# SSM quarters reordered, u and y stored in the chain's layout, gate weights on GpSimd's queue: a hybrid encoder block on Trainium2

## The chip, the cores and the metric

The kernel runs on one core of one Trainium2 chip. A core has five engines, each with an instruction stream of its own that it works through in order: TensorE (PE: matmuls and transposes, with its weight loads listed as PEld), VectorE (DVE), ScalarE (ACT), GpSimd (POOL) and SyncE (SP, which here only issues DMAs). ACT and POOL can issue DMAs too. The metric is the device time of one execution in microseconds; lower is better.

## What is computed

One encoder layer over 16 meta tokens and 1024 inputs of width 1024 (L = 1040 rows), in float32. The part that the change touches is the state-space branch ("SSM") and the sigmoid gates beside it:

```python
xn = _rmsnorm(h, norm_mix_g)
q, k, v, f_logit, u, gates = jnp.split(xn @ w_in, SPLITS, axis=-1)
y_a = _forgetting_attention(q, k, v, f_logit, b_forget) @ w_attn_out
z = jax.nn.gelu(_s5(u, ...))              # 32 groups of 16 channels, 64 complex states each
zg = z @ w_glu
y_s = zg[..., :D_MODEL] * sigmoid(zg[..., D_MODEL:])
g = sigmoid(gates)
h = h + (g[..., :D_MODEL] * y_a + g[..., D_MODEL:] * y_s) @ w_o
h = h + _conv_ffn(_rmsnorm(h, norm_ffn_g), ...)
out = _rmsnorm(h, norm_final_g)[:, N_META:]

def _s5(u):                               # x_t = lam_bar * x_(t-1) + b_bar u_t,  y = Re(C x_t) + D u_t
    _, states = lax.associative_scan(combine, (a, bu), axis=0)
    return einsum('gcp,lbgp->blgc', cmat, states).real + d_skip * u
```

## The kernel before

Every float32 matrix product is made of float32r pieces: an operand is split into a rounded part (`hi`) and the rest (`lo`), and three products are summed (`dense_steps`, L139 to L143). A weight block of 1024 x 128 passes `wchunk` (L127): one load into `raw` by SP, a rounding copy to `whi`, and a subtraction to `wlo` on GpSimd (`split_lo`, L124). With `act=True` the rounding copy is ACT's (L133).

The program is written in a tile framework. The code's order is a priority; a planner with its own estimates of durations makes each engine's final order before the run, and adds the semaphores. A tile with a tag has a fixed number of buffers (`bufs`), and a new tile of that tag waits until an older one is done with. A pool that is closed gives its SBUF to later pools, whose tiles wait for those that they lie on. `after(inst, first)` orders two instructions on one engine.

In order of time, the part of the kernel up to the attention does this:

1. Rows are normalised (`norm_rows`, L152), transposed on PE and split into `xhi` and `xlo` (`to_feature`, L162). The square of each row tile is ACT's (L155), as is the copy into `xhi` (L169).
2. `u_proj` (L300) projects u, 128 channels at a time, from weights split in `u_weights` (L263), and stores it to DRAM as `u_d`, [512 channels, 8, 130]: a sequence of 1040 rows is 130 chunks of CH = 8 rows.
3. `ssm` (L1176) first works out powers and rotations in small DVE steps, then does four quarters of 8 groups each. For quarter q, `tables(q)` (L1426) makes Gm (DVE), Kt (PE, then ACT copies it, L1448), Tm (Kt sent eight times by SP into a Toeplitz form, L1456, after GpSimd cleared it, L1454) and Wi (DVE, PE, ACT). `chain(q)` (L1474) loads U from `u_d` in eight pieces (SP, L1482), multiplies by Wi (L1489), ACT copies the result to wr and wi (L1492, L1493), DVE rotates, scans (L1504, L1505) and rotates back into St, PE makes Y from Tm and U (L1522) and from Gm and St (L1523), ACT copies Y out, applies GELU (L1526) and issues eight stores to `y_d` (L1528).
4. `gate_chunk` (L344) makes the sigmoid gates of the SSM branch, eight chunks of 72 matmuls, each result of 128 x 1026 stored to `g_d` by ACT (L361). These matmuls are what PE can do while the quarters go round.
5. `load_z` (L434) reads `y_d` back, one load of 128 channels each (SP, L439), splits z and makes the sums and differences that the GLU's products use (L444 to L462; GpSimd makes one of them, L455).
6. `project_qk(0)` (L375) and `forget` (L409, with weights loaded in `forget_w`, L324) run on PE, then the GLU (`glu`, L465, whose products are in `seven`, L175, at L194 to L196).

After that come values, attention, the output projection and the feed-forward part, which the change does not touch.

The order of step 3 in the code is `tables(0)`, `chain(0)`, `tables(1)`, `chain(1)`, then `u_proj(2)`, and the same for quarters 2 and 3 (L314 to L336). In a chain the wr and wi copies come first and the output last, so in the code the copies of quarter q+1 come behind the output of quarter q.

Of the kernel before, what the change touches and what calls it, by code (L numbers as in the profile page):

```python
# [47 lines left out]
def block_kernel(ctx, tc, x, meta, g1, w_in, b_f, w_ao, l_re, l_im, b_re, b_im, c_re, c_im,  # L48
# [78 lines left out]
    def wchunk(src, k, eng=None, act=False):  # L127
        raw = wp.tile([P, k, P], F, tag="raw", name="raw", padded_shape=[P, KD, P])
        SY.dma_start(raw, src.rearrange("(k p) m -> p k m", p=P))
        hi = wp.tile([P, k, P], R, tag="whi", name="whi", padded_shape=[P, KD, P])  # L130
        lo = wp.tile([P, k, P], R, tag="wlo", name="wlo", padded_shape=[P, KD, P])
        if act:
            S.copy(hi, raw)  # L133
# [18 lines left out]
    def norm_rows(pl, src, n, gB, xs):  # L152
        sq = pl.tile([P, D], BF, tag="sq", name="sq")
        ss = pl.tile([P, 1], F, tag="ss", name="ss", bufs=3)
        S.activation(sq[:n], src, AF.Square, accum_out=ss[:n])  # L155
        va = pl.tile([P, 1], F, tag="vr", name="vr", bufs=3)
        v_ = V.tensor_scalar(va[:n], ss[:n], 1.0 / D, EPS, ALU.mult, ALU.add)
        rs = pl.tile([P, 1], F, tag="rs", name="rs", bufs=3)
        GP.tensor_tensor(rs[:n], va[:n], nhalf[:n], ALU.pow)
        return v_, V.scalar_tensor_tensor(out=xs[:n], in0=src, scalar=rs[:n], in1=gB[:n], op0=ALU.mult, op1=ALU.mult)  # L160

    def to_feature(xs, n, dhi, dlo, col, bank=st_ps):  # L162
        for hf in range(2):
# [5 lines left out]
            S.copy(ho, t3[:, :, :n])  # L169
            split_lo(V, dlo[:, 4 * hf:4 * hf + 4, col:col + n], t3[:, :, :n], ho)  # L170

    def m_ps():
# [101 lines left out]
    S.dma_start(g1B, g1.partition_broadcast(P))  # L274
    ssm_log, ssm_loads, ssm_steps = ssm(tc, sp, st_ps, ident, u_d, y_d, l_re, l_im, b_re, b_im, c_re, c_im, d_sk, l_dt)
    xts = [sp.tile([P, D], F, tag=tag, name="xt", bufs=n) for tag, n in (("sy", 3), ("Gm", 2), ("Wi", 2), ("U", 2))
# [23 lines left out]
    def u_proj(m0):  # L300
# [29 lines left out]

    u_proj(2)
    forget_w()
    st_u.close()
    for q in range(2, 4):
        ssm_tables(q)
        ssm_chain(q)  # L336


    st_g = ExitStack()
    gp_ = pool(st_g, "gates", side="right")  # L340

    okeep = {}

    def gate_chunk(i, pl, tanh):  # L344
        c0 = 3 * AW + H + SW + P * i
        whi, wlo = wchunk(w_in[:, c0:c0 + P], KD, GP, act=not tanh)
        gs = pl.tile([P, LQ], F, tag="gs", name="gs", bufs=1 if tanh else 2)
        for t, n in QBLK:
            ps = mm_ps()
            yield from dense_steps(ps[:, :n], whi, wlo, xhi[:, :, T0 + t:T0 + t + n],  # L350
                                   xlo[:, :, T0 + t:T0 + t + n], KD)
            if tanh:
                S.activation(gs[:, t:t + n], ps[:, :n], AF.Tanh, scale=0.5)
            else:
                S.activation(gs[:, t:t + n], ps[:, :n], AF.Sigmoid)
        if tanh:
            GP.tensor_scalar(gs, gs, 0.5, 0.5, ALU.mult, ALU.add)
        if pl is not gp_ and i == KD - 1:
            okeep["g"] = gs
        else:  # L360
            (SY if tanh else S).dma_start(g_d[P * i:P * i + P], gs)  # L361

    for i in range(KD, 2 * KD):
        run(gate_chunk(i, gp_, False))
    st_g.close()
    st_s.close()

# [66 lines left out]
    def load_z():  # L434
        zts = []
        for m in range(4):
            tag = "gl" if m % 2 else "ms"
            zt = gz.tile([P, CH, NCH], F, tag=tag, name="zt", bufs=2)
            SY.dma_start(zt, y_d[P * m:P * m + P])  # L439
            zts.append(zt)  # L440
# [59 lines left out]

    n_used = [0]
    T4 = load_z()
    qk = qk_tiles(0)
    run(project_qk(0, qk))
# [670 lines left out]

def ssm(tc, sp, s_ps, ident, u_d, y_d, l_re, l_im, b_re, b_im, c_re, c_im, d_sk, l_dt):  # L1176
    nc = tc.nc
# [21 lines left out]

    lraw = sm([G, 2, 2, NS])  # L1200
    for i, src in enumerate((l_re, l_im)):
# [24 lines left out]
    def rest():  # L1226
# [21 lines left out]
        def expf(o, a):  # L1248
            n, r, t, e = sm(W), sm(W), sm(W), sm(W, dt=I32)
            TS(n, a, 1.4426950408889634, None, ALU.mult)  # L1250
# [15 lines left out]
        def cmul(or_, oi, ar, ai, br, bi, t, u):  # L1266
# [6 lines left out]
            V.tensor_copy(or_, t)  # L1273

        dt_ = sm(W)
        expf(dt_, ldt)
# [40 lines left out]
        TT(pi[:, 1], rad, ei, ALU.mult)  # L1317
        w1, w2 = sm([P, 4, G]), sm([P, 4, G])
# [107 lines left out]
        def tables(qt):  # L1426
# [47 lines left out]
        def chain(qt):  # L1474
            g0 = qt * GQ
            Gm, Tm, Wi, dt8 = state.pop(qt)
            if qt == 1:
                rot.append(rotation(1))
            rc, rs = (t_[:, qt % 2 * HQ:qt % 2 * HQ + HQ] for t_ in rot[qt // 2])
            U = big("U", [P, GQ, NCH])  # L1480
            for j in range(CH):
                SY.dma_start(U[16 * (7 - j):16 * (8 - j)],  # L1482
                             u_d[g0 * GC:(g0 + GQ) * GC, j, :].rearrange("(g c) n -> c g n", c=GC))
            wr, wi, ta, tb = (big(n, [P, HQ, NCH]) for n in ("wr", "wi", "ta", "tb"))
            for e in range(2):
                for q in range(0, HQ, 2):
# [5 lines left out]
                    S.copy(wr[64 * e:64 * e + 64, q:q + 2], w3[:64])  # L1492
                    S.copy(wi[64 * e:64 * e + 64, q:q + 2], w3[64:])  # L1493
            TT(ta, wr, rc, ALU.mult)
            TT(tb, wi, rs, ALU.mult)
# [13 lines left out]
            for part, (op, fa, fb) in enumerate(((ALU.subtract, wr, ta), (ALU.add, ta, wr))):  # L1509
# [3 lines left out]
                for e in range(2):  # L1513
                    r_ = slice(64 * e, 64 * e + 64)
                    TT(S4[64 * part:64 * part + 64, :, e, 1:], x_[r_, :, :NCH - 1], y_[r_, :, :NCH - 1], op)
            Y = big("sy", [P, GQ, NCH], "Y")
            for q in range(0, GQ, 3):
                nq = min(3, GQ - q)
                yps = s_ps()
                for i in range(nq):  # L1520
                    yo = yps[:, NCH * i:NCH * i + NCH]
                    PE.matmul(yo, Tm[:, q + i, :], U[:, q + i, :], start=True, stop=False)  # L1522
                    PE.matmul(yo, Gm[:, q + i, 1:, :].rearrange("p t c -> p (t c)"), St[:, q + i, :],  # L1523
                              start=False, stop=True)
                S.copy(Y[:, q:q + nq].rearrange("p a n -> p (a n)"), yps[:, :NCH * nq])
            S.activation(Y, Y, AF.Gelu_apprx_tanh)  # L1526
            for j in range(CH):
                S.dma_start(y_d[g0 * GC:(g0 + GQ) * GC, j, :].rearrange("(g c) n -> c g n", c=GC),  # L1528
                            Y[16 * j:16 * j + 16])

# [31 lines left out]
```

## Time and profile before

| | us |
|---|---|
| median of 3 runs | 1583.6 |
| lowest and highest | 1581.55, 1585.9 |
| the profiled execution's own time | 1581.32 |
| its span in the profile | 1579.3 |

| engine | busy us | share of the span |
|---|---|---|
| PE | 1474.3 | 93% |
| DVE | 1095.5 | 69% |
| POOL | 752.0 | 48% |
| ACT | 661.5 | 42% |

The profile is of one execution. It gives each instruction's start and end on its engine, and, for the time an engine stood still, the instruction whose end released it (`<-`). `x8` is a count. A name such as `zt<-y_d` is the tile written and the one read, L439 the line of the kernel before, `SPq` and `ACTq` the issuing of DMAs by those engines. A view by windows gives the busy time of each engine within a stretch and the TensorE clock that was granted there, as a share of full speed. PE busy at a low clock does less work in the same time. GpSimd's spans are rough.

### The profile page before, as it was taken

How to read it: one execution, taken by the hardware profiler on the slowest of the kernel's cores; microseconds unless marked ns; L12 is line 12 of the kernel's file. 1: busy time of each engine (PE TensorE's matmuls, PEld its weight loads, DVE VectorE, ACT ScalarE, POOL GpSimd, SP SyncE). 2: the span in 40 equal slices, each digit the busy share in tenths (PEclk: the TensorE clock that was granted, in tenths of full speed). 3: DMA queues.
4: the chain of work that ended last, by engine and by line, in shares of the span. 5: the costliest groups of instructions: out<-in, count | busy, mean ns of one | idle time of the engine just before them, and what ended most of it. 6: DMA issues, size and time to landing. Idle time of an engine off the chain costs nothing.

```text
span 1579.3 us, 25961 instructions
## 1 busy us (share of the span) xinstructions
PE 1474.3 (93%) x9649; PEld 1378.3 (87%) x9649; DVE 1095.5 (69%) x2248; ACT 661.5 (42%) x1278; POOL 752.0 (48%) x780
## 2 busy tenths in 40 slices
PE   5999987899999989999999899999999998899996
PEld 5899886898899979999778899999999997677875
DVE  6999648783466656647335887777777766998886
ACT  5133336542355646542123444444444444342443
POOL 5312215753355445535110643333333338799796
PEclk9999998999999999999999999999999999989997
DMA  8465632454122233137442012222222232841202
GB/s 204 87 90 102 110 71 72 137 161 92 41 56 57 61 38 71 51 123 243 165 120 81 27 55 81 81 81 81 81 81 81 81 120 98 303 141 40 74 1 107
DMA packets 154353, 151.80 MB, mean 96 GB/s; under 512 B 23065, under 2 KB 123161, under 8 KB 154227
## 3 DMA queue, kind: packets, MB, share of 16 engines
q1 hardware_dynamic: 145971, 137.36, 32.1%
q10 hardware_dynamic: 8096, 12.73, 2.5%
q8 instruction: 76, 1.25, 0.3%
q14 instruction: 50, 0.41, 0.1%
q0 software_dynamic: 160, 0.05, 0.0%
HBM read 111.04 MB, written 37.90 MB: 94 GB/s over the span
## 4 chain that ended last, share of the span: by engine, by line
PE 62%; DVE 14%; POOL 9%; DMA 6%; issue 5%; ACT 2%; SPq 1%; ACTq 0%; POOLq 0%; DVEq 0%
PE sp L195 4%; PE sp L196 4%; PE sp L194 4%; PE mm L143 4%; PE mm L141 4%; PE mm L142 4%; PE tp L195 3%; PE tp L194 3%; PE tp L196 3%; PE mm L194 3%; PE mm L195 3%; PE mm L196 3%; PE tp L652 2%; PE po L674 2%; PE po L673 2%
## 5 line engine op out<-in xcount | busy, mean ns | idle before, releaser
L141 PE MATMUL mm<-xhi,whi 128*128 128x342 f32 (+2 forms) x584 | 193.7, 332 | 12.6 <-DVE q L125 6.9
L143 PE MATMUL mm<-xhi,wlo 128*128 128x342 f32 (+2 forms) x584 | 191.8, 329 | 0.0
L142 PE MATMUL mm<-xlo,whi 128*128 128x342 f32 (+2 forms) x584 | 191.3, 328 | 0.0
L141 PEld LDWEIGHTS mm<-xhi,whi 128*128 128x128 f32 x584 | 112.3, 192 | 14.1 <-issue 6.3
L923 POOL TENSOR_TENSOR ov<-ov,og 128x1024 f32<-128x1024 f32 x21 | 51.8, 2465 | 142.4 <-ACT og L922 139.6
L142 PEld LDWEIGHTS mm<-xlo,whi 128*128 128x128 f32 x584 | 112.2, 192 | 0.6 <-issue 0.2
L143 PEld LDWEIGHTS mm<-xhi,wlo 128*128 128x128 f32 x584 | 111.8, 192 | 1.0 <-issue 0.6
L125 POOL TENSOR_TENSOR wlo<-raw,whi 128x1024 fp32r<-128x1024 f32 x24 | 64.0, 2668 | 74.3 <-ACT whi L133 74.0
L912 ACT CAST sw<-sf 128x512 fp32r<-128x512 f32 x76 | 47.4, 624 | 108.2 <-POOL sf L918 68.4
L125 DVE TENSOR_TENSOR sw<-sf,sw 128x512 fp32r<-128x512 f32 x76 | 57.1, 751 | 50.1 <-ACT sw L912 50.1
L659 ACT CAST th<-tp 128x256 fp32r<-128x256 f32 (+3 forms) x120 | 56.1, 472 | 72.6 <-PE tp L652 29.0
L194 PE MATMUL mm<-xhi,sw 128*128 128x256 f32 (+1 forms) x304 | 85.4, 281 | 0.8 <-DVE ov L947 0.8
L912 ACT CAST sw<-raw 128x512 fp32r<-128x512 f32 x69 | 42.4, 620 | 103.5 <-DMA raw<-in_w_ffn_up_dram 36.5
L196 PE MATMUL mm<-xhi,sw 128*128 128x256 f32 (+1 forms) x304 | 85.5, 281 | 0.0
L195 PE MATMUL mm<-xlo,sw 128*128 128x256 f32 (+1 forms) x304 | 85.2, 280 | 0.0
L125 DVE TENSOR_TENSOR tl<-tp,th 128x256 fp32r<-128x256 f32 (+3 forms) x120 | 65.2, 547 | 26.2 <-ACT th L659 24.3
L918 POOL TENSOR_TENSOR sf<-raw 128x512 f32<-128x512 f32 x38 | 49.7, 1308 | 52.9 <-DMA raw<-in_w_ffn_up_dram 24.4
L624 POOL TENSOR_SCALAR pt<-pt,nm 128x144 f32<-128x144 f32 (+4 forms) x72 | 50.8, 707 | 44.1 <-DVE nm L623 42.8
L918 POOL TENSOR_TENSOR sf<-raw,sf 128x512 f32<-128x512 f32 x38 | 49.8, 1312 | 41.2 <-DVE sw L125 41.2
L622 ACT ACTIVATE pt<-pt,nm 128x144 f32<-128x144 f32 (+4 forms) x72 | 52.9, 735 | 28.5 <-DVE nm L621 27.9
L673 PE MATMUL po<-th,vt 128*128 128x256 f32 (+1 forms) x200 | 57.2, 301 | 8.0 <-DVE nm L620 7.9
L981 DVE SCALAR_TENSOR_TENSOR ov<-hv,cwt,ov 128x1024 f32<-128x1024 f32 x38 | 62.9, 1655 | 0.1
(598 smaller groups left out, 5516.0 us busy)
## 6 DMA issues: line engine op xcount, KB each, us to landing
raw<-in_w_ffn_up_dram SPq DMA_DIRECT2D x44, 512.0 KB, 3.9
raw<-in_w_in_dram SPq DMA_DIRECT2D x28, 512.0 KB, 8.3
ar<-a_d SPq DMA_DIRECT2D x44, 256.0 KB, 4.3
wr<-in_w_ffn_down_dram SPq DMA_DIRECT2D x44, 256.0 KB, 3.5
a_d<-ov SPq DMA_DIRECT2D x21, 512.0 KB, 2.6
fb<-f_d SPq DMA_DIRECT2D x8, 520.0 KB, 5.0
g_d<-gs ACTq DMA_DIRECT2D x8, 513.0 KB, 4.8
gl<-g_d SPq DMA_DIRECT2D x8, 513.0 KB, 4.3
```

Of the source, the lines that this page charges most:

```text
L125: return eng.tensor_tensor(out_, src, hi.bitcast(F), ALU.subtract)
L141: yield PE.matmul(ps, whi[:, i, :], ahi[:, i], start=(i == 0), stop=False)
L142: yield PE.matmul(ps, whi[:, i, :], alo[:, i], start=False, stop=False)
L143: yield PE.matmul(ps, wlo[:, i, :], ahi[:, i], start=False, stop=(i == k - 1))
L194: PE.matmul(ps, a[0][:, i], bh, start=(i == 0 and not joins), stop=False, skip_group_check=True)
L195: PE.matmul(ps, a[0][:, i], bl, start=False, stop=False, skip_group_check=True)
L196: PE.matmul(ps, a[1][:, i], bh, start=False, stop=(i == kh - 1), skip_group_check=True)
L659: S.copy(th[:kn, z:tw], tp[:kn, z:tw])
L673: PE.matmul(po[:, :w], vt[:kn, kk, h, :], th[:kn, gi * w:gi * w + w], start=(kk == 0), stop=False)
L912: S.copy(hi, src)
L918: GP.tensor_tensor(f_, a, b, op)
L981: V.scalar_tensor_tensor(out=o, in0=h_[:, j:SEQ + j], scalar=cwc(j, m), in1=o, op0=ALU.mult, op1=ALU.add)
```

## The change

- **Layout.** `u_d` and `y_d` become [4 quarters, 128, 8 groups, 130], where the 128 are (row in chunk, channel in group): the layout that a chain works in. U is then one load per quarter and Y one store (before: eight each). The stores of u become 8 per 128 channels, issued by SP (before: one, by ACT), and the loads of z 8 per 128 channels (before: one).
- **Row order in a chunk.** U and Tm now have the rows of a chunk in natural order, before they were reversed; Wi uses reversed powers `qr` and `qi`, made by 16 small GpSimd copies.
- **Order of the quarters.** `chain` becomes a generator that stops after the wr and wi copies. `begin(q)` runs `tables(q)` and that first part. The code's order is now begin(0), begin(1), `u_proj(2)`, the rest of chain 0, begin(2), the rest of chain 1, begin(3), the rests of chains 2 and 3. Within Y the product with St comes first. The second half of the rotation table is made behind chain 0's last state.
- **Gate weights.** `wchunk` with `act=True`, that is the eight gate chunks, loads `raw` by GpSimd's queue. Each third of a gate chunk is stored as soon as it is ready (24 stores in place of 8), from tiles a third as large.
- **Start.** The rounding copies of the u weights go from GpSimd to ACT, and the square of row tile 3 is ordered behind the `xhi` copies of the three tiles ahead.
- **Memory.** `lraw`, the power helpers w1 and w2, and the temporaries of `expf` share buffers with other tiles; the forget gate's weights take the place of the gates' pool and are loaded behind `load_z`.

The diff, cut to its core:

```diff
-    u_d = dp.tile([SW, CH, NCH], F, name="u_d")
-    y_d = dp.tile([SW, CH, NCH], F, name="y_d")
+    u_d = dp.tile([SW // P, P, P // GC, NCH], F, name="u_d")
+    y_d = dp.tile([SW // P, P, P // GC, NCH], F, name="y_d")
...
     def wchunk(src, k, eng=None, act=False):
-        SY.dma_start(raw, src.rearrange("(k p) m -> p k m", p=P))
+        (GP if act else SY).dma_start(raw, src.rearrange("(k p) m -> p k m", p=P))
...
     def u_weights(m):
-            GP.tensor_scalar(hi[:, sl], src, 1.0, 0.0, ALU.mult, ALU.add)
+            S.copy(hi[:, sl], src)
...
+    done = []
     for i, (t, n) in enumerate(TILES):
         xt = xts[i - 1] if i else xm
-        norm_rows(n1, xt[:n], n, g1B, xt)
-        to_feature(xt, n, xhi, xlo, t, rot)
+        sq_ = norm_rows(n1, xt[:n], n, g1B, xt)
+        if i == 3:
+            for cp_ in done:
+                after(sq_, cp_)
+        done += to_feature(xt, n, xhi, xlo, t, rot)
...
     def u_proj(m0):
         for m in (m0, m0 + 1):
-            S.dma_start(u_d[P * m:P * (m + 1)], us[m])
+            um = u_d[m].rearrange("(j c) g n -> g c j n", c=GC)
+            for g in range(P // GC):
+                SY.dma_start(um[g], us[m][GC * g:GC * g + GC])
+    chains = {}
+    def begin(q):
+        ssm_tables(q)
+        chains[q] = ssm_chain(q)
+        next(chains[q])
     u_proj(0)
-    for q in range(2):
-        ssm_tables(q)
-        ssm_chain(q)
+    begin(0)
+    begin(1)
     u_proj(2)
-    forget_w()
+    for q in range(4):
+        run(chains[q])
+        if q < 2:
+            begin(q + 2)
     st_u.close()
-    for q in range(2, 4):
-        ssm_tables(q)
-        ssm_chain(q)
...
     def gate_chunk(i, pl, tanh):
             else:
-                S.activation(gs[:, t:t + n], ps[:, :n], AF.Sigmoid)
+                gs = pl.tile([P, LQ // 3], F, tag="gs", name="gs", bufs=2)
+                S.activation(gs, ps[:, :n], AF.Sigmoid)
+                S.dma_start(g_d[P * i:P * i + P, t:t + n], gs)
...
     def load_z():
-            SY.dma_start(zt, y_d[P * m:P * m + P])
+            ym = y_d[m].rearrange("(j c) g n -> g c j n", c=GC)
+            for g in range(GQ):
+                SY.dma_start(zt[GC * g:GC * g + GC], ym[g])
...
     T4 = load_z()
+    forget_w()
...
+        qr, qi = sm([P, CH, G]), sm([P, CH, G])
+        for j in range(CH):
+            GP.tensor_copy(qr[:, j], pr[:, CH - 1 - j])
+            GP.tensor_copy(qi[:, j], pi[:, CH - 1 - j])
...
         def tables(qt):
-                SY.dma_start(Tm[16 * (7 - j):16 * (8 - j), :, 16 * j:], Kt[:, :, :P - 16 * j])
+                SY.dma_start(Tm[16 * j:16 * (j + 1), :, 16 * j:], Kt[:, :, :P - 16 * j])
-            TT(Vm, bcx(bA, CH), bcp(pr, CH), ALU.mult)
-            TT(tv, bcx(bB, CH), bcp(pi, CH), ALU.mult)
+            TT(Vm, bcx(bA, CH), bcp(qr, CH), ALU.mult)
+            TT(tv, bcx(bB, CH), bcp(qi, CH), ALU.mult)
...
         def chain(qt):
-            if qt == 1:
-                rot.append(rotation(1))
-            for j in range(CH):
-                SY.dma_start(U[16 * (7 - j):16 * (8 - j)],
-                             u_d[g0 * GC:(g0 + GQ) * GC, j, :].rearrange("(g c) n -> c g n", c=GC))
+            SY.dma_start(U, u_d[qt])
...
+            yield
...
+            if qt == 0:
+                n_ = len(log)
+                rot.append(rotation(1))
+                after(log[n_], log[n_ - 1])
...
-            for j in range(CH):
-                S.dma_start(y_d[g0 * GC:(g0 + GQ) * GC, j, :].rearrange("(g c) n -> c g n", c=GC),
-                            Y[16 * j:16 * j + 16])
+            S.dma_start(y_d[qt], Y)
```

More of the change, by code (lines that the diff above doesn't have):

```diff
@@ L311, in u_proj, with gate_chunk @@
         for m in (m0, m0 + 1):
-            S.dma_start(u_d[P * m:P * (m + 1)], us[m])
-    u_proj(0)
-    for q in range(2):
-        ssm_tables(q)
-        ssm_chain(q)
+            um = u_d[m].rearrange("(j c) g n -> g c j n", c=GC)
[6 more added lines that the diff above has]
+        next(chains[q])
+    u_proj(0)
+    begin(0)
+    begin(1)
+    u_proj(2)
+    for q in range(4):
+        run(chains[q])
+        if q < 2:
+            begin(q + 2)
+    st_u.close()
+    st_g = ExitStack()
+    gp_ = pool(st_g, "gates", side="right")
+    okeep = {}
+    def gate_chunk(i, pl, tanh):
+        c0 = 3 * AW + H + SW + P * i
+        whi, wlo = wchunk(w_in[:, c0:c0 + P], KD, GP, act=not tanh)
+        if tanh:
+            gs = pl.tile([P, LQ], F, tag="gs", name="gs", bufs=1)
+        for t, n in QBLK:
+            ps = mm_ps()
+            yield from dense_steps(ps[:, :n], whi, wlo, xhi[:, :, T0 + t:T0 + t + n],
+                                   xlo[:, :, T0 + t:T0 + t + n], KD)
+            if tanh:
+                S.activation(gs[:, t:t + n], ps[:, :n], AF.Tanh, scale=0.5)
+            else:
+                gs = pl.tile([P, LQ // 3], F, tag="gs", name="gs", bufs=2)
+                S.activation(gs, ps[:, :n], AF.Sigmoid)
+                S.dma_start(g_d[P * i:P * i + P, t:t + n], gs)
+        if tanh:
+            GP.tensor_scalar(gs, gs, 0.5, 0.5, ALU.mult, ALU.add)
+            if pl is not gp_ and i == KD - 1:
+                okeep["g"] = gs
+            else:
+                SY.dma_start(g_d[P * i:P * i + P], gs)
+    for i in range(KD, 2 * KD):
+        run(gate_chunk(i, gp_, False))
+    st_g.close()
+    st_s.close()
     st_f = ExitStack()
@@ L1317, in rest @@
         TT(pi[:, 1], rad, ei, ALU.mult)
[L1318 removed]
+        w1, w2 = (big(n, [P, 4, G], n) for n in ("ta", "tb"))
         for q in (1, 2, 4):
```

55 lines of the change are left out of this document (17 added, 38 removed).

## The prediction

> **What bounds the kernel now.** I read the page first: TensorE (PE) is busy 93% of the span, so a change pays only where PE stands still or runs at a reduced clock. The profiled execution took 1581.32 us, 2.0 us more than its span:
>
> ```profile
> span 1579.3 us, 25961 instructions
> ```
>
> Next the stage windows (per engine: busy us, instruction count; then the granted PE clock):
>
> ```profile
> core 0: us, PE busy (x) PEld busy (x) DVE busy (x) ACT busy (x) POOL busy (x), PEclk, DMA share, GB/s
> 20.00:72.00 52.00, 49.26 (x318) 48.80 (x319) 48.65 (x209) 17.67 (x36) 17.35 (x29) 1.00 0.58 124
> 72.00:92.00 20.00, 14.78 (x78) 13.19 (x77) 20.00 (x54) 6.41 (x9) 6.53 (x2) 0.83 0.48 95
> 92.00:229.00 137.00, 132.26 (x883) 127.39 (x882) 102.92 (x165) 50.82 (x96) 30.42 (x17) 0.99 0.53 92
> 229.00:240.00 11.00, 5.08 (x35) 4.89 (x35) 2.26 (x5) 6.31 (x12) 0.34 (x1) 0.78 0.28 48
> 240.00:252.00 12.00, 12.00 (x69) 11.68 (x69) 10.26 (x13) 9.44 (x11) 6.40 (x2) 0.91 0.47 179
> 252.00:266.60 14.60, 6.69 (x27) 4.37 (x24) 11.42 (x13) 8.06 (x18) 11.09 (x6) 0.65 0.12 36
> 266.60:275.00 8.40, 6.97 (x54) 6.55 (x55) 8.37 (x16) 4.31 (x10) 4.07 (x2) 1.00 0.01 2
> 275.00:295.00 20.00, 14.94 (x97) 14.02 (x96) 11.71 (x20) 11.81 (x24) 13.46 (x14) 0.83 0.28 85
> ```
>
> Until 229 us the gate matmuls keep PE full while the four SSM quarters go round DVE, ACT and the queues; after 229 there is a hole. Busy time times granted clock is work at full clock. From 229 to 266.6 that is 5.08 x 0.78 + 12.00 x 0.91 + 6.69 x 0.65 = 4.0 + 10.9 + 4.3 = 19.2 us of work in 37.6 us: **18.4 us lost**. From 266.6 to 295 another 1.4 + 7.6 = 9.0 us are lost. The hole is 27.4 us in all.
>
> Then the waits of PE (total us, times, longest) name what ends the hole's stalls:
>
> ```profile
> PE mm L416 <- DVE kl L125: 7.8, 1, 7.8
> PE mm L141 <- DVE q L125: 5.9, 1, 5.9
> PE mm L141 <- ACT xhi L169: 5.6, 1, 5.6
> ```
>
> The 5.9 us fall in the window 229:240, where PE is busy 5.08 of 11.00. PE runs the q/k projection, its PSUM banks fill, and ACT, which empties them, is behind the fourth quarter's output (ACT's timeline: start, us):
>
> ```profile
> 230.64 1.28 ACT L1526 ACT_TABLE_LOAD   x1
> 231.93 1.07 ACT L1526 ACTIVATE Y<-Y 128x1040 f32<-128x1040 f32 x1
> 233.03 3.70 ACTq L1528 DMA_DIRECT2D y_d<-Y  x8
> 236.77 0.38 ACT L384 CAST q<-mm 64x272 fp32r<-64x272 f32 x1 [3.77 <-DMA y_d<-Y]
> ```
>
> The chain of waits runs on through the reload of y; there GpSimd's difference (L455, 10.57 us beside a DVE that hardly pauses) holds ACT, and so PE a second time (the 7.8 us):
>
> ```profile
> 236.28 2.41 DMA y_d<-Y
> 239.09 3.32 DMA zt<-y_d
> ...
> 246.35 10.57 POOL zf L455
> 256.94 0.62 ACT z3h L461
> ```
>
> PE's timeline gives the point at which the GLU takes over with z:
>
> ```profile
> 266.57 0.36 PE L194 MATMUL mm<-zhi,ops 128*128 128x260 f32 x1 [0.15 <-DVE kl L125]
> ```
>
> So the time is set by the end of quarter 3, its way through y_d, and z. How much earlier can that end be? DVE is busy 102.92 of 137 us in 92:229, that is 34.1 us idle, and its waits say where:
>
> ```profile
> DVE Kt L1187 <- ACT Kt L1448: 17.7, 3, 11.1
> DVE ta L1187 <- ACT wr L1492: 10.6, 2, 5.7
> ```
>
> Both are ACT copies for the next quarter that stand in order behind the output of the one ahead; ACT's own wait:
>
> ```profile
> ACT Kt L1448 <- DMA y_d<-Y: 11.9, 3, 5.2
> ```
>
> **The change part by part.** *(a) Order of the quarters.* Tables, U load, Wi products and wr/wi copies of quarter q+1 now come ahead of quarter q's scan and output. The two waits, 28.3 us, can go. What can still stand before a copy is one GELU with a table load to each side, 1.28 + 1.07 + 1.28 = 3.6 us, so I take 24.7 us. Bounds: 11.9 us (only ACT's hold at the eight issues goes) and 34.1 us (all idle time).
>
> *(b) Sixteen reversing copies on GpSimd (qr, qi).* No row shows a 128x32 copy there; the nearest is a 128x64 one:
>
> ```profile
> L328 POOL TENSOR_SCALAR wf<-fraw 128x64 fp32r<-128x64 f32 x1 | 0.2, 243 | 7.0 <-DMA fraw<-in_w_in_dram 7.0
> ```
>
> 16 x 0.243 = 3.9 us. They cost nothing beside a GpSimd that is 6.53 of 20 us busy, or up to these 3.9 us where DVE, full there (20.00 of 20), waits for the powers or is held up; I take 2.
>
> *(c) Transfers.* Duration of one issue in ns (min/median/max), from the lines' own views:
>
> ```profile
> L439 SPq DMA_DIRECT2D zt<-y_d x4: 344/400/424, 239.1 to 240.4; - x4
> ```
> ```profile
> L1528 ACTq DMA_DIRECT2D y_d<-Y x32: 309/442/465, 125.7 to 236.3; - x32
> ```
> ```profile
> L1482 SPq DMA_DIRECT2D U<-u_d x32: 302/428/849, 53.1 to 165.5; - x32
> ```
> ```profile
> L361 ACTq DMA_DIRECT2D g_d<-gs x8: 326/344/352, 104.5 to 214.5; - x8
> ```
>
> y out: 8 issues become 1, 3.70 us become 0.44: **-3.3 us** on the path. u: before, 4 stores on ACT and 32 loads on SP; now 32 stores and 4 loads on SP. Per quarter the path has eight small issues and one large either way (8 x 0.428), nothing; what stands behind them on SP are Tm's loads, and the gate weights leave that queue. z in: 4 issues become 32, 12.8 us for 1.6: **+11.2 us** if all wait for the last output, +1.6 if the first three quarters are ahead. Before, none was ahead (SP's wait):
>
> ```profile
> SPq L439 <- DMA y_d<-Y: 19.9, 2, 19.3
> ```
>
> though three quarters of y were long in DRAM; so zt's place in SBUF, or the order, held them. With an SSM pool laid out anew part of that can go: I take 6.4. The gates' stores are 24 issues for 8, 16 x 0.344 = 5.5 us more on an ACT busy 50.82 of 137: hidden. Half-size gs buffers give a store two thirds of a chunk, some 10 us, to land: hidden.
>
> *(d) Gate weights on GpSimd's queue.* The issues that this queue shows (ns), and its other work per chunk:
>
> ```profile
> L1203 POOL DMA_DIRECT2D sm<-in_ssm_lambda_im_dram x2: 496/504/512, 2.5 to 3.4; - x2
> ```
> ```profile
> L1205 POOL DMA_DIRECT2D sm<-in_ssm_log_dt_dram x1: 571/571/571, 3.9 to 3.9; - x1
> ```
> ```profile
> L125 POOL TENSOR_TENSOR wlo<-raw,whi 128x1024 fp32r<-128x1024 f32 x10 | 30.5, 3046 | 74.2 <-ACT whi L133 74.0
> L1454 POOL MEMSET Tm<- 128x1024 f32 x4 | 3.8, 953 | 10.4 <-PE tp L1522 6.6 <-PE sp L1522 3.9
> ```
>
> A weight load has 1024 rows; these have 32 and 128. Ends: 1.2 us (0.07 us per 96 rows more) and 16 us (32 times 0.50). I take 4.6, eight times the nearer row. A chunk lasts (214.5 - 104.5)/7 = 15.7 us; 4.6 + 3.05 + half a clear of Tm 0.5 = 8.2 us fit, and two raw buffers run ahead: nothing. What waits behind a load is the split; what a load can wait behind is Tm's clear, held 6.6 and 3.9 us by PE. The Trainium skill, "SBUF — State Buffer", section "SBUF: two separate sides", speaks against this part: a DMA issued by GpSimd starves while DVE runs in a two-port mode, 620 ns becoming some 3100 ns. The long DVE copy of that kind here is short and rare:
>
> ```profile
> L1470 DVE COPY dt<-sm 128x520 f32<-128x520 f32 x4 | 1.7, 422 | 0.0
> ```
>
> By the page's figure the load would take GpSimd some 3.1 us (an estimate), and the sum would stay; what the rule makes of the time beyond that is the starved rival below.
>
> *(e) Start.* ACT's squares stood before the copies that PE wanted:
>
> ```profile
> 19.69 1.06 ACT L155 ACTIVATE sq<-xt 128x1024 bf16<-128x1024 f32 x1 [4.58 <-DMA xt<-in_x_dram]
> ```
> ```profile
> 22.74 0.79 PE L141 MATMUL mm<-xhi,whi 128*128 128x272 f32 x2 [5.64 <-ACT xhi L169]
> ```
>
> With the square of tile 3 behind those copies PE can begin up to 5.6 us earlier; then it needs tiles that land no earlier, so I take **2.0**. ACT's hi copies of the u weights lie in its idle time (17.67 of 52 busy).
>
> *(f) Forget gate loads* now follow z's loads on SP; they land behind the projection of q and k (10.9 us of work in 240:252 alone), and cost PE their delay only if z's loads are still waiting then. *(g)* PE's losses at 72:92, 20 - 14.78 x 0.83 = 7.7 us, come from DVE being full; the second tables now go first, the work is the same: nothing, bounds 7.7 either way.
>
> **The sum.** Quarter 3's last state ended here:
>
> ```profile
> 226.01 1.41 DVE L1187 TENSOR_TENSOR St<-ta,wr 64x516 f32<-64x516 f32 x2
> ```
>
> at 227.4, its y landed at 236.28 + 2.41 = 238.7. After: 24.7 + 3.3 - 2 = 26.0 us earlier. With z's loads z is 26.0 - 6.4 = 19.6 us earlier: GLU possible at 266.6 - 19.6 = 247.0. PE alone, without the hole: 229 - 2.0 + 19.2 = 246.2. z is later by 0.8, so the GLU begins at 247.0 and everything behind is **19.6 us** earlier; the 9.0 us after 266.6 I leave in place. Own time 1581.3 - 19.6 = 1561.7; against the median of 1583.6, which lies 2.3 above it: **1564.0 us**. Two limits within 0.8 us of each other also say that more than this needs both to improve.
>
> **Rivals.** *z stays last.* The 32 loads all queue behind the last output and the quarters gain less: between 11.9 + 3.3 - 2 - 11.2 = 2.0 and 24.7 + 3.3 - 2 - 11.2 = 14.8 us, middle 8.4: **1575**. For it: SP's 19.3 us wait; against: DVE's 34.1 us of idle time.
>
> *The whole hole closes.* 27.4 + 5.6 = 33.0 us: **1551**. For it: every stall in it starts with ACT behind the output; against: L455 depends on DVE's density, not on the quarter's end.
>
> *Slower: GpSimd's queue starves PE of gate weights.* At 16 us a load, a chunk takes 16 + 3.05 + 0.5 = 19.5 us for 15.7, eight times 3.8 = 31 us: 1564 + 31 = **1595**. It costs nothing below 12.2 us a load, eats the gain at 12.2 + 19.6/8 = 14.6, and is slower by over 0.3% from 15.2. For it: nothing in the trace shows a 1024-row load there, and DVE is busy three quarters of the stage; against: 128 rows cost hardly more than 32, and each load has most of two chunks' time in hand. The page named under (d) states such a hold; the trace so far shows neither the hold nor its absence, since its five small issues fell beside a nearly idle DVE.
>
> *The order isn't what the code suggests*: the planner lays the queues by its own estimates and ACT's copies stay behind; only the issue counts change, 11.9 + 3.3 - 2 - 11.2 = 2.0 us: **1582**, no change.
>
> **How the numbers follow.** Forecast 0.50, z last 0.20 (a fifth of it within 0.3%), whole hole 0.12, starved 0.10, order unchanged 0.08. 0.3%, 4.8 us, is about what a measurement of this kernel can tell from no change. Faster 0.50 + 0.16 + 0.12 = 0.78, same 0.04 + 0.08 = 0.12, slower 0.10. The range holds forecast, z last and the closed hole, 0.82: 1551 to 1580.
>
> **What would show it.** Right: DVE's waits on Kt and wr gone, last St near 205, one y_d issue per quarter, PE's 5.9 us wait gone, first L194 near 247. Wrong: PE waiting on whi or wlo during the gates, GpSimd's issues above 12 us, SP issuing zt only behind the last y_d, or the L455 stall moving under the GLU.

## The result and the profile after

| | before | after |
|---|---|---|
| median, us | 1582.57 (4 runs, 1578.97 to 1585.9) | 1564.51 (4 runs, 1564.06 to 1565.77) |
| profiled execution, us | 1581.32 | 1565.77 |

The ratio is **0.9888, with a 95% interval of 0.9864 to 0.9911**: of 1582.57 us that is 14.1 to 21.5 us saved, 17.7 in the middle. The forecast was 19.6 us and 1564.0. The two profiled executions differ by 15.55 us. Single executions of one kernel scatter by some 3 us to each side, so sizes below come from ratios, and places from traces.

Line numbers are those of each kernel: L198 and L200 of after are L194 and L196 of before, L1210 is the helper L1187, L461 is L439. First the windows of after, with the columns of those of before (busy us and count by engine, PE clock, DMA share, GB/s):

```profile
20.00:72.00 52.00, 49.78 (x310) 48.17 (x311) 48.53 (x203) 20.56 (x43) 21.03 (x34) 0.92 0.56 117
72.00:92.00 20.00, 15.80 (x94) 14.12 (x93) 20.00 (x62) 5.08 (x8) 8.48 (x4) 0.91 0.34 58
92.00:229.00 137.00, 129.04 (x873) 126.18 (x872) 106.85 (x171) 60.64 (x105) 29.81 (x19) 0.98 0.62 109
229.00:240.00 11.00, 10.19 (x66) 9.90 (x65) 8.89 (x10) 6.68 (x9) 7.84 (x5) 1.00 0.57 127
240.00:257.50 17.50, 13.85 (x70) 11.29 (x70) 15.44 (x25) 11.81 (x29) 11.07 (x9) 0.80 0.11 32
257.50:275.00 17.50, 14.44 (x116) 13.82 (x115) 11.55 (x20) 12.03 (x23) 9.96 (x9) 1.00 0.20 56
275.00:285.90 10.90, 10.84 (x90) 10.61 (x89) 8.39 (x18) 5.42 (x16) 8.37 (x11) 1.00 0.71 203
```

The hole ahead of the GLU lost 18.4 us of full-clock work. Now 229 to 257.5 loses 0.8 + (17.5 - 13.85 x 0.80) = 7.2, and what lies behind, 257.5 to 285.9, 3.1 instead of the 9.0 of before. The hole has gone from 27.4 to 10.3 us.

DVE's waits, and its timeline at the last state (start, us):

```profile
DVE zf L476 <- DMA zt<-y_d: 19.3, 1, 19.3
DVE ta L1210 <- ACT wr L1516: 8.7, 2, 8.3
```
```profile
199.99 1.42 DVE L1210 TENSOR_TENSOR St<-ta,wr 64x516 f32<-64x516 f32 x2
```

The Kt wait of 17.7 us has gone from the list, and the largest wait is now for z, which comes when the quarters are done. The last state ends at 201.4 instead of 227.4. From there on the lead shrinks. ACT's timeline, SP's, and the chain of waits:

```profile
207.68 0.33 ACTq L1558 DMA_DIRECT2D y_d<-Y  x1
237.17 2.20 ACT L466 CAST zhi<-zt 128x1040 fp32r<-128x1040 f32 x1
```
```profile
204.65 26.39 SPq L461 DMA_DIRECT2D zt<-y_d  x32
```
```profile
207.68 8.43 DMA y_d<-Y
...
218.44 3.33 DMA zt<-y_d
```

One issue of 0.33 us has taken the place of eight, as forecast, but the store, of eight times the bytes, took 8.43 us to land, where the last of the eight took 2.41. Of the 32 loads of z only six had been issued when the last output landed (207.68 + 8.43 = 216.1); the last was issued at 231.0. SP's waits ahead of these loads ended more with the load of k's weights and with Y's product on PE than with y itself:

```profile
SPq L461 <- DMA raw<-in_w_in_dram: 5.2, 1, 5.2
SPq L461 <- PE tp L1555: 3.4, 1, 3.4
SPq L461 <- DMA y_d<-Y: 2.0, 1, 2.0
```

PE's timeline where the GLU begins:

```profile
257.34 0.34 PE L437 MATMUL mm<-xlo,wf 128*64 128x384 f32 x1
257.52 0.28 PE L198 MATMUL mm<-zhi,ops 128*128 128x260 f32 x1
```

PE goes from the forget gate's last product (L437) into the GLU without a gap, and by DVE's line view z was whole by then:

```profile
L126 DVE TENSOR_TENSOR zlo<-zf,zhi x2: 693/844/996, 236.3 to 250.1; 128x520 fp32r<-128x520 f32 x2
```

This last split of z, started at 250.1, is done at 251.1. z was no longer what the GLU waited for; PE came later. (In before this last split started only at 270.7, behind the GLU's first product.) The GLU's products on the tile z1h (min/median/max ns, start of the first and of the last) show how long the GLU then takes, in before and in after:

```profile
L196 PE MATMUL tp<-z1h,ops x32: 279/282/420, 271.7 to 354.1; 128*128 128x260 f32 x32
```
```profile
L200 PE MATMUL tp<-z1h,ops x32: 277/282/287, 260.6 to 338.5; 128*128 128x260 f32 x32
```

From the first to the last it is 82.4 us before and 77.9 after. The lead along the way:

| point | before | after | earlier by |
|---|---|---|---|
| last St ends | 227.4 | 201.4 | 26.0 |
| y landed | 238.7 | 216.1 | 22.6 |
| last issue of z ends | 240.9 | 231.0 | 9.9 |
| first GLU product | 266.57 | 257.52 | 9.05 |
| last GLU product on z1h | 354.1 | 338.5 | 15.6 |
| profiled time | 1581.32 | 1565.77 | 15.55 |

### The profile page after: what moved, and what is told of

It reads as the page before. It is cut to its first block, busy times and chain, and to the rows that moved or that the text cites. A ratio compares the mean times of both kernels' runs of the same rounds, so it can differ in the third digit from the quotient of the medians.

```text
span 1564.0 us, 26066 instructions
## 1 busy us (share of the span) xinstructions
PE 1467.3 (94%) x9649; PEld 1372.1 (88%) x9649; DVE 1088.5 (70%) x2248; ACT 667.8 (43%) x1295; POOL 751.4 (48%) x788
## 4 chain that ended last, share of the span: by engine, by line
PE 62%; DVE 15%; POOL 7%; DMA 7%; issue 4%; ACT 3%; SPq 1%; ACTq 0%; POOLq 0%; DVEq 0%
PE sp L199 4%; PE sp L198 4%; PE sp L200 4%; PE mm L144 4%; PE mm L142 4%; PE mm L143 4%; PE tp L198 3%; PE tp L199 3%; PE tp L200 3%; PE mm L200 3%; PE mm L198 3%; PE mm L199 3%; PE tp L675 2%; PE po L697 1%; PE po L696 1%
## 5 line engine op out<-in xcount | busy, mean ns | idle before, releaser
L198 PE MATMUL mm<-xhi,sw 128*128 128x256 f32 (+1 forms) x304 | 85.4, 281 | 0.8 <-DVE ov L970 0.8
L200 PE MATMUL mm<-xhi,sw 128*128 128x256 f32 (+1 forms) x304 | 85.5, 281 | 0.0
```

The costliest lines, as they stand in the source:

```text
L198: PE.matmul(ps, a[0][:, i], bh, start=(i == 0 and not joins), stop=False, skip_group_check=True)
L200: PE.matmul(ps, a[1][:, i], bh, start=False, stop=(i == kh - 1), skip_group_check=True)
```

## The experiments

All were timed in five rounds beside the kernel before, whose medians were 1581.0 to 1582.0. A variant of after that ends near 0.9888 has lost nothing. After its expectation stands each result, as ratio and 95% interval.

### Order and layout of y, one at a time and together

**e1**, the old order of the quarters in an otherwise new kernel:

```diff
-    begin(0); begin(1); u_proj(2); for q in range(4): run(chains[q]) ...
+    for q in range(2): begin(q); run(chains[q])
+    u_proj(2)
+    for q in range(2, 4): begin(q); run(chains[q])
```

> The kernel after, with the quarters in the old order: tables, chain and output of one quarter before the next one's tables, u_proj(2) between quarters 1 and 2. Layouts, queues, stores and start stay as after. Theory A (the order is what brings the gain): last St back from 201.4 to within 5 us of 227, DVE waits for ACT's Kt copy again (15 us or more in sum), the GLU starts near 266 and the time is 1576 to 1585. Rival B (one U load, one Y store and the weights' new queue bring it): last St stays before 212 and the time stays below 1570.

Measured: 0.9944 (0.9928 to 0.9961), 1572.66 us. DVE's waits show that the old stall is back on wr, and partly on Kt:

```profile
DVE ta L1210 <- ACT wr L1516: 18.7, 2, 11.0
DVE Kt L1210 <- ACT Kt L1477: 5.0, 2, 4.6
```

The order frees DVE, as forecast, and the last state ends at 223.5 instead of 201.4; but these 22 us of lead are worth 0.9944 - 0.9888, 8.9 us, of time. Neither theory had that number: half of the gain stays without the order. Where the 22 us went shows in the GLU:

```profile
L200 PE MATMUL tp<-z1h,ops x32: 279/283/420, 250.5 to 345.1; 128*128 128x260 f32 x32
```
```profile
L126 DVE TENSOR_TENSOR zlo<-zf,zhi x2: 678/688/699, 254.7 to 265.1; 128x520 fp32r<-128x520 f32 x2
```

PE came to the GLU sooner than in after (250.5 for 260.6) and took 94.6 us over it instead of 77.9, since z was whole only at 265.8. Ahead of the GLU PE has no hole at all in e1:

```profile
229.00:240.00 11.00, 11.00 (x71) 11.00 (x70) 8.50 (x16) 9.91 (x22) 1.53 (x2) 1.00 0.52 132
240.00:249.30 9.30, 9.30 (x60) 8.04 (x59) 7.15 (x10) 7.92 (x13) 6.30 (x5) 1.00 0.75 166
```

The splits of z cost DVE time ahead of the GLU or under it; the last products on z1h differ by 6.6 us, not by 22.

**e2**, `y_d` in the old layout, with eight stores by ACT and four loads by SP:

```diff
-            S.dma_start(y_d[qt], Y)
+            for j in range(CH):
+                S.dma_start(y_d[g0*GC:(g0+GQ)*GC, j, :].rearrange("(g c) n -> c g n", c=GC),
+                            Y[16*j:16*j+16])
```

> The kernel after, with y in DRAM as before: eight stores per quarter by ACT, four loads of z by SP. Theory A (the 32 loads of z, 26.4 us on SP, and y's 8.43 us to land hold the second half of z, and with it DVE and PE between 237 and 257.5): zt is loaded by about 222, the last zhi copy is 8 to 12 us earlier than 237.2, PE's losses between 240 and 257.5 (6.0 us) go mostly, time 1558 to 1561. Rival B (PE's own queue sets the GLU's start, z comes in time anyway): 1563 to 1566. Rival C (the eight issues on ACT stand in the way of the gates' sigmoids and the next quarter's copies): 1567 or more, last St later than 204.

Measured: 0.9953 (0.9936 to 0.9970), 1574.6 us: it costs 10 us, three times what issues can cost. ACT's timeline shows why:

```profile
214.02 0.46 ACT L361 ACTIVATE gs<-po 128x342 f32<-128x342 f32 x1 [10.70 <-DMA g_d<-gs]
214.93 0.49 ACT L1554 COPY Y<-tp 128x390 f32<-128x390 f32 x1 [0.45 <-ACT gs L361]
```

A sigmoid stands ahead of the last Y copies and waits 10.70 us for a gate store to free its buffer. ACT works in order, so Y waits too (after copied it at 202.9). z was whole at 256.5 all the same, ahead of the GLU's first product at 269.0: what PE lost here it lost to the sigmoids themselves and to what came behind them. Its two longest waits:

```profile
PE mm L142 <- ACT gs L361: 4.4, 1, 4.4
PE mm L142 <- DVE q L126: 3.5, 1, 3.5
```

The gate store was slow while the DMA engines were busy. First the row of e2, then that of after, around the last stores of the gates and the load of k's weights:

```profile
200.00:215.00 15.00, 14.73 (x102) 14.34 (x101) 1.22 (x2) 0.98 (x3) 3.44 (x2) 1.00 0.76 66
198.00:213.00 15.00, 14.75 (x103) 14.36 (x102) 3.33 (x4) 6.36 (x9) 4.13 (x3) 1.00 0.91 78
```

The engines are 76% and 91% busy for 66 and 78 GB/s. A weight block is 1024 rows of 512 bytes; in the window of after, the queue that carries it takes 80.6% of the engines' time for 0.62 MB. The 8.43 us of the y store above have the same place. That the load delays the gate store of e2 is argued from this; e8 below tests it for y and z.

**e10**, both edits at once:

> Old order of the quarters and y's old layout; u's layout, the gate weights' queue, the thirds of gates and the start as after. With the old order and the new layout it was 1572.7. Theory A (z's loads by quarter, the first ones ahead of the last output, are what was left of the gain there): all loads of z wait for the last output again, 1578 to 1583, as before. Rival B (the smaller gate stores, the one U load or the start brought it): 1570 to 1575.

Measured: 0.9950 (0.9936 to 0.9964), 1574.21 us. SP's waits:

```profile
SPq L459 <- DMA y_d<-Y: 17.9, 2, 13.0
```

The loads of z wait for the last output again, as in before, and yet the time is that of e1. So the two parts don't add: under the old order the layout is worth nothing that can be measured (0.9944 against 0.9950), under the new one 10 us; under the old layout the order is worth nothing (0.9950 against 0.9953), under the new one 8.9. Together they are worth some 10 us (0.9950 against 0.9888).

### What decides between the quarters' end and the GLU

**e5**, four small gate buffers (`name="gs", bufs=2` becomes `bufs=4`), nothing else:

> The kernel after, with four small buffers for a gate's thirds in place of two. Theory A (the stores of the gates, 10 to 14 us when a weight load has the DMA engines, hold the sigmoid that needs their buffer, in after 4.0 and 1.5 us, on PE's path only through PSUM, which PE had to spare there): within 2 us of 1564.5, ACT's wait for g_d gone. Rival B (that wait delays the gates' end and so the projection behind them): 1559 to 1562.

Measured: 0.9889 (0.9873 to 0.9905), 1566.13 us: no change; ACT waited for a gate store as long as in after.

**e6**, e2 and e5 together:

> The previous experiment on y's old layout, with four small buffers for the gates. Theory A (there a sigmoid waited 10.7 us for a store of a gate, ahead of the last Y copy on ACT; with more buffers that hold goes, and what is left is the layout alone): first zhi copy near 215 in place of 225.4, time 1561 to 1566. Rival B (the eight issues and the wait behind them are the cost): still 1570 or more.

Measured: 0.9928 (0.9911 to 0.9946), 1571.74 us, between e2 and after. ACT's hold is gone (Y copied at 203.9) and the last `zhi` copy from z's loads starts 11.5 us before that of after, at 225.7. Still the GLU began at 260.5. GpSimd's timeline, then PE's waits:

```profile
207.35 1.04 POOL L136 TENSOR_SCALAR whi<-raw 128x1024 fp32r<-128x1024 f32 x1 [9.87 <-issue]
223.66 2.50 POOL L475 TENSOR_TENSOR zf<-zt 128x520 f32<-128x520 f32 x1 [12.79 <-DMA zt<-y_d]
226.12 10.82 POOL L136 TENSOR_SCALAR whi<-raw 128x1024 fp32r<-128x1024 f32 x1
```
```profile
PE po L142 <- POOL whi L136: 6.9, 1, 6.9
```

The split of k's weights stands behind z's difference (L475) on GpSimd and then takes 10.82 us for what took 1.04, beside a DVE that is full:

```profile
226.00:237.00 11.00, 4.09 (x25) 3.77 (x23) 10.94 (x11) 4.81 (x7) 10.93 (x2) 0.84 0.09 15
```

PE is busy 4.09 of these 11 us, at a clock of 0.84. Here an early z cost PE its weights.

**e8**, k's weight load ordered behind z's last load on SP, to give z the DMA engines:

```diff
     def wchunk(src, k, eng=None, act=False, behind=None):
-        (GP if act else SY).dma_start(raw, ...)
+        ld = (GP if act else SY).dma_start(raw, ...)
+        if behind is not None:
+            after(ld, behind)
```

> The kernel after, with the load of the first k weights (1024 pieces of 512 bytes) ordered on SP behind the loads of z. Theory A (this load, issued at 198.7, has the DMA engines until about 212, with 97.8% of their time at 50 GB/s, and both the last y store, 8.4 us for 2.4 before, and z's first loads, 9.4 us, stand behind it): the last y store lands in under 4 us, the first zhi copy is 4 to 8 us earlier than 220.7, the last one earlier than 231, and the time is 1558 to 1561, if the k weights then come by about 240. Rival B (z's own small loads fill the engines): the store still takes 6 us or more, no gain. Rival C (the k weights come too late): PE waits for them at 238 to 245, 1565 to 1572.

Measured: 0.9940 (0.9924 to 0.9956), 1573.9 us. ACT's timeline and PE's waits:

```profile
216.12 1.27 ACT L471 CAST zhi<-zt 128x520 fp32r<-128x520 f32 x1 [1.70 <-DMA zt<-y_d]
```
```profile
PE po L144 <- POOL whi L138: 11.6, 1, 11.6
```

With that load out of the way z's loads land in at most 4.1 us instead of 9.5; the last y store, issued at 209.24, releases SP at 212.3, after 3.1 us instead of 8.43; and the first `zhi` copy starts 4.5 us earlier. So the weight load does hold y and z. But the last `zhi` copy starts only 1.9 us earlier (235.26 for 237.17), and PE waits 11.6 us for k, whose load, issued at 230.64, takes 12.6 us to land. The time is lost there.

**e9**, e6 with the splits of q's and k's weights ahead of z, and GpSimd's difference ordered behind k's:

```diff
+    early = [wchunk(w_in[:, w*AW:w*AW+P], KD, GP) for w in range(2)]
     T4 = load_z()
...
+            after(GP.tensor_tensor(f3, ...), kept[0])
```

> The kernel with y's old layout and four gate buffers (the sixth experiment), with the split of the first q and k weights placed ahead of z's loading, and GpSimd's difference for z ordered behind the k split. There the rounding copy of the k weights took GpSimd 10.8 us for 1.05, beside a DVE that formed z, and PE waited 9.1 us for these weights. Theory A (that copy, behind z's difference and beside a full DVE, is what undid the early z): PE's waits for whi and wlo go, the GLU starts 6 to 10 us earlier than 260.5, time 1560 to 1565. Rival B (DVE and GpSimd only change places: what GpSimd does first, it now does last, and z is late): GLU start within 3 us of 260.5, time 1569 or more.

Measured: 0.9888 (0.9872 to 0.9905), 1563.57 us. GpSimd's timeline has k's split ahead and short again:

```profile
221.48 1.81 POOL L138 TENSOR_SCALAR whi<-raw 128x1024 fp32r<-128x1024 f32 x1 [7.66 <-PE po L145]
225.98 2.48 POOL L477 TENSOR_TENSOR zf<-zt 128x520 f32<-128x520 f32 x1 [0.19 <-DMA zt<-y_d]
```

With the sigmoid no longer holding ACT and z's difference no longer holding k's weights, the old layout of y ends where the new one does. So the 10 us of e2 are these two holds and not the layout as such. (Under the new layout four buffers alone bring nothing, by e5; the early splits alone weren't run there.) PE's waits on these weights are gone, yet it is no faster than after: the GLU began at 258.4, with z whole at 253.4. The time is that of theory A, the GLU's start that of rival B.

### The parts that cost and bring nothing

**e3**, gate weights on SP's queue again: `(GP if act else SY).dma_start(raw` becomes `SY.dma_start(raw`.

> The kernel after, with the gate weights loaded by SP again. Theory A (a load costs GpSimd 0.9 us, hidden, and takes nothing from anyone; the queue as such is neutral): within 2 us of 1564.5. Rival B (on SP the loads stand, waiting for a weight buffer, ahead of u's stores, Tm's and z's loads, so the quarters and z come later): 1567 to 1575, last St later than 204. Rival C (on SP they come earlier, since GpSimd no longer has its splits ahead of them): PE's waits shrink, 1560 to 1562.

Measured: 0.9889 (0.9875 to 0.9904), 1563.38 us: no change.

**e4**, the old start:

```diff
-        if i == 3:
-            for cp_ in done:
-                after(sq_, cp_)
...
-            S.copy(hi[:, sl], src)
+            GP.tensor_scalar(hi[:, sl], src, 1.0, 0.0, ALU.mult, ALU.add)
```

> The kernel after, with the start as before: rounding copies of u's weights by GpSimd, no order between the square of tile 3 and the copies into xhi. Theory A (the new start loses PE 2.0 us more up to 60 us, and nothing absorbs it): 1561.5 to 1563.5, PE's loss up to 60 us down by 2. Rival B (PE has slack behind it, chain 0's output at 110 to 130 waits for DVE anyway): 1564 to 1565.5. Rival C (the new start does what it was taken for): 1566.5 or more.

Measured: 0.9901 (0.9885 to 0.9916), 1565.03 us: no difference that can be told, though PE's wait of 5.4 us on `xhi` is back.

**e7**, `u_d` in the old layout, with its one store by ACT for each 128 channels and eight loads of U by SP for each quarter:

```diff
-            SY.dma_start(U, u_d[qt])
+            for j in range(CH):
+                SY.dma_start(U[16*j:16*(j+1)], u_d[g0*GC:(g0+GQ)*GC, j, :].rearrange("(g c) n -> c g n", c=GC))
```

> The kernel after, with u in DRAM as before: one store per 128 channels by ACT, eight loads of U per quarter by SP. Theory A (neutral, eight small issues stand on SP either way): within 2.5 us of 1564.5. Rival B (the 32 stores of u on SP hold Tm's loads of the first quarters, and chain 0 starts at 105.6 for 99.2): chain 0 starts 4 to 6 us earlier and the time is 1559 to 1561.

Measured: 0.9887 (0.9867 to 0.9907), 1565.47 us: no change.

### Where the rest of the gain lies

**e11**, the kernel before with one part alone: gate results in thirds, each stored when ready.

```diff
+                gs = pl.tile([P, LQ // 3], F, tag="gs", name="gs", bufs=2)
+                S.activation(gs, ps[:, :n], AF.Sigmoid)
+                S.dma_start(g_d[P * i:P * i + P, t:t + n], gs)
```

> The kernel before with one part of the change alone: the gates' results in tiles of a third, each stored as soon as it is ready. Old order and old layouts together with the other parts of the change took 1574.2, some 8 us less than the kernel before, and the old u, the old weights' queue and the old start made no difference after the change. Theory A (the smaller stores and buffers are what is left): 1572 to 1576. Rival B (it is the place and time of the forget gate's weights, or several parts together): 1580 to 1584.

Measured: 0.9949 (0.9936 to 0.9962), 1572.92 us: 8.1 us for a part that the prediction counted as nothing. The windows show where it begins; 72:92 in e11:

```profile
72.00:92.00 20.00, 17.40 (x109) 15.82 (x108) 20.00 (x54) 7.96 (x14) 7.58 (x2) 0.91 0.56 110
```

PE was busy 14.78 us at 0.83 there in before. GpSimd's and DVE's timelines, before:

```profile
84.20 2.46 POOL L125 TENSOR_TENSOR wlo<-raw,whi 128x1024 fp32r<-128x1024 f32 x1 [6.46 <-ACT whi L133]
```
```profile
84.35 2.46 DVE L1187 TENSOR_TENSOR Kt<-Kt,dg 16x128 f32<-16x128 f32 x1
87.03 1.21 DVE L1187 TENSOR_TENSOR Vm<-Vm,tv 128x1024 f32<-128x1024 f32 x1
```

and in e11:

```profile
84.15 0.27 DVE L1190 TENSOR_TENSOR Kt<-Kt,dg 16x128 f32<-16x128 f32 x1
84.64 1.21 DVE L1190 TENSOR_TENSOR Vm<-Vm,tv 128x1024 f32<-128x1024 f32 x1
```

A DVE operation of 0.27 us takes 2.46 when it starts 0.15 us behind GpSimd's subtraction, and Vm comes 2.4 us later. The Trainium skill, "SBUF — State Buffer", section "SBUF: two separate sides", states that DVE and GpSimd share one pair of ports under an exclusive lock, which a DVE operation with two SBUF inputs needs beside a GpSimd operation that reads SBUF, and that whoever starts first has it for its whole instruction; the 2.46 us agree. The last state ends 5.0 us earlier (222.4) and the GLU begins at 258.6. But that one collision is no more than 2.4 us of this.

**e12**, e11 with the forget gate's weights moved to their new place, behind z's loads (`st_f` and `forget_w()` below `load_z()`):

> The kernel before with the thirds of the gates and the forget gate's weights moved behind the gates and the loads of z. Theory A (thirds alone bring it): as the run with the thirds alone. Theory B (the forget gate's place brings it): 1572 to 1576 here, 1580 to 1584 with the thirds alone. Rival C (neither; it is the sum of small things, or the order that the planner falls into): 1579 to 1584 in both.

Measured: 1.0005 (0.9995 to 1.0016), 1581.99 us: the gain is gone. In 72:92:

```profile
72.00:92.00 20.00, 15.06 (x82) 13.31 (x81) 20.00 (x58) 5.88 (x9) 6.58 (x2) 0.86 0.46 92
```

PE is back at 15.06 us, though it needs the moved weights only at 252.3, and another small DVE operation is caught beside the same subtraction (GpSimd, 85.20 to 87.61):

```profile
85.29 2.48 DVE L1190 TENSOR_TENSOR pc<-rt 128x128 f32<-128x128 f32 x1
```

DVE's order differs from e11's from 9 us on: the planner has laid another plan. e11's is close to that of before, with the same order on DVE up to 45 us and on GpSimd up to 149 us. Since e12 has the thirds too, the 8 us of e11 can't be credited to them as such. Whether the other plan or the later loads take them back, and how the moved loads lead the planner to it, wasn't settled.

## Why the prediction was right, and where it was wrong

The total came out right, and the sum's two halves did not: the GLU began 10.5 us later than forecast (257.5 for 247.0), and 5.9 of the 9.0 us of loss "left in place" behind it went away. So the closeness of 1564.5 to 1564.0 is in part luck. The two profiled executions differ by 15.55 us, 4 less than the 19.6 forecast; the medians lie closer to it.

- **(a) Order.** Right in its mechanism. 24.7 us less the 2 of (b) was 22.7 forecast at the last state; 26.0 measured, of which e1 shows 22.1 to be the order's. DVE stood idle 33.8 us between 92 and the last state before, 10.5 after. "The two waits can go" holds for one of them: Kt's has gone, wr's is 8.7 for 10.6. In time the order is worth 8.9 us (e1), and only beside the new layout (e10 against e2).
- **(b)** The reversing copies were hidden: in their line views nothing waits for them, and the last starts at 64.7 us. Their medians are 314 and 219 ns for the 243 taken:

```profile
L1350 POOL COPY sm<-sm x8: 226/314/1344, 4.6 to 62.2; 128x32 f32<-128x32 f32 x8
L1351 POOL COPY sm<-sm x8: 204/219/268, 4.8 to 64.7; 128x32 f32<-128x32 f32 x8
```

- **(c) y out.** -3.3 us for the issues was right in itself (0.33 us), but the term had no landing in it: 8.43 - 2.41 = 6.0 us came back as one store beside k's weights (3.1 us without them, e8). **z in.** The term was mis-sized: the last issue came 14.9 us behind y's landing instead of 2.2, 12.7 us worse for the 6.4 taken and the 11.2 of its bound. With 26 of 32 issues behind the last y, its own sign "SP issuing zt only behind the last y_d" had for the most part come. u was nothing, as forecast (e7). The gates' stores, "some 10 us, to land: hidden", were hidden in after, where a sigmoid waits 4.0 us for one, and not in e2, where one waits 10.70.
- **(d) Gate weights on GpSimd.** Nothing, as forecast (e3). The issues, by the line view of after:

```profile
L130 POOL DMA_DIRECT2D raw<-in_w_in_dram x8: 902/902/962, 63.5 to 160.7; - x8
```

  That is below the low end, 1.2 us, and the loads landed in 9.3 us in the median, by SP (e3) in 12.0. The starved rival didn't come. The rule of the same section of the Trainium skill, that a DMA from GpSimd's queue can't write its descriptors while DVE runs an operation in a two-port mode, for which it names an fp32 copy within SBUF, left no mark here; but DVE's copies between 60 and 200 us are 6 us in sum, so the run hardly tests it.
- **(e) Start.** Wrong: 0.2 us, not 2.0. PE's first product came at 22.52 for 22.74. The wait on `xhi` has gone, but a wait on one of DVE's small SSM steps stands in its place:

```profile
20.73 1.11 PE L170 MATMUL tp<-ident,xt 128*128 128x128 f32 x4 [5.47 <-DVE sm L1234]
```

  In 20:72 PE did 49.78 x 0.92 = 45.8 us of work for 49.3; the low clock there doesn't come with the start as such, since kernels with the same start were granted 1.00 (e3, e5, e7) or 0.92 (e6, e10). e4 shows that the whole part is worth nothing that can be measured.
- **(f)** The moved loads were hidden, as costed. What wasn't in the term is that such a move gives another plan: e12 and e11 differ by this move alone and by 9 us.
- **(g)** 7.7 us of loss at 72:92 became 20 - 15.80 x 0.91 = 5.6.
- **The step that failed is "PE alone, without the hole: 246.2".** The prediction saw two limits within 0.8 us, z and PE, and gave PE's side the whole hole back, as if z's arrival cost PE nothing. Measured, z was whole at 251.1, 4.1 us behind its forecast, and PE came at 257.5, 11.3 behind its own. Of these 11.3 us, 7.2 are left in the hole (windows above), 2.0 are the start, and 2.1 would have to lie ahead of 229. The windows there show 5.9 us less work than before (3.5 less in 20:72, 4.5 less in 92:229, 2.1 more in 72:92), and with clocks given to two digits the account doesn't close. In 240:257.5 DVE is busy 15.44 of 17.5 us, with z's splits among those for q and k, and PE waits for the latter:

```profile
PE mm L436 <- DVE q L126: 1.9, 1, 1.9
PE po L436 <- DVE kl L126: 1.8, 1, 1.8
```

  These waits are 3.7 of the 6.4 us lost in 240:257.5; the rest is the clock of 0.80. In e1, where much of z's splitting comes later, PE is busy from 229 to the GLU without a pause, at full clock (rows under e1), and is there at 249.3, near the forecast.
- **The 9.0 us left in place** came down to 3.1, and this is the other side of the same error: what z's splits take from PE ahead of the GLU they no longer take under it. The nine kernels with the new order need 77.6 to 78.4 us from the first to the last product on z1h, the five with the old one (before, e1, e10, e11, e12) 82.4 to 94.6. In all nine z was whole ahead of the GLU's first product, in all five only behind it. That is how the two errors came to cancel in part: 10.5 us lost ahead, 5.9 gained behind.

The four named rivals: "z stays last" priced z's loads at 11.2 us, near the 12.7 measured, but z wasn't the last. "The whole hole closes" got 17.1 of 27.4 us. Starvation and an unchanged order did not occur.

What the runs settle: after, e3, e5, e7 and e9 end between 0.9887 and 0.9889 with different layouts, queues and buffers, all with z whole ahead of PE: there PE, and no longer the quarters, sets the GLU's start, at 255.5 to 261.2. Falling off this level takes a hold: the quarters' end, under the GLU (e1), or, ahead of it, ACT behind a gate store (e2) and k's weights (e6, e8). Some 8 of the 17.7 us come without order and layout (e10, 0.9950), and their cause is open: the share that the thirds have within the whole change wasn't tried. Open is also why e1, e10 and e11 end at one level, 0.9944 to 0.9950: a plan without the stall at 72:92 would explain it, and is not shown. No version beat after by what can be measured.

## What to carry to other kernels

When a stage is freed early, work out which engine the freed work now crowds and when the next limit is reached, here PE behind a full DVE, before the lead is counted as time: 22 us were worth 9. A part that is undone alone shows what it is worth beside the others, and order and layout were worth some 10 us together and nothing one without the other. Where a planner lays the order, an edit costed at nothing can come with another plan and with 0.5% of the time, so a part's worth needs the trace of its plan beside its time.

## What the hardware showed unexpectedly

- A GpSimd copy of 1.04 us took 10.82 us beside a DVE busy 10.94 of 11 us (e6), and a subtraction of 0.7 to 1.6 us took 8.72 in e9. It loses more than one instruction's time: nine DVE operations ran one behind the other during the 10.82 us.
- With a load of 1024 rows of 512 bytes on its way the DMA engines were 91% busy at 78 GB/s, and a y store of 520 KB took 8.43 us to land; with that load moved away (e8) it took 3.1.
- A load of 1024 rows cost GpSimd's queue 0.90 to 0.96 us to issue, less than twice the 0.50 to 0.57 of 32 and 128 rows.
